# Two block levels of the scan's inverses on TensorE, and TensorE in program order

## The chip, the cores and the metric

The kernel runs on one core of a Trainium2 chip. The metric is the device time of one launch in microseconds; the time before is 3900.61 us, the median of three runs (3896.09 to 3906.93). The engines go by the profile's names: PE is TensorE (matmul, PEld its weight loads), DVE VectorE, ACT ScalarE, POOL GpSimd, SP the engine that issues most DMAs. Each works through its own list of instructions in order, and semaphores hold an instruction back until what it reads is there.

## What the kernel computes

A trunk of two layers over 512 latent and 256 context tokens of width 1024. Each layer is a half-weighted SwiGLU, a token mixer, and another SwiGLU; the second layer's mixer is a bidirectional RWKV-7, and only its recurrence is touched here. Of the reference:

```
def step(s, inp):                       # rwkv_scan, per head, both directions
    dec, kt, vt, kkt, bt = inp[:5]
    sa = jnp.einsum('bhvk,bhk->bhv', s, kkt)
    s = s * dec[:, :, None, :] - sa[..., None] * bt[:, :, None, :] \
        + vt[..., None] * kt[:, :, None, :]
    y = jnp.einsum('bhvk,bhk->bhv', s, inp[5]) if with_out else None
    return s, y
```

Sixteen heads of width 64; every latent scan starts from the final context state of its direction.

## The kernel before

The function `rwkv_scan` (L1181) does the recurrence in chunks of 64 tokens. Inside a chunk the dependence of each token on those before it is a triangular 64x64 matrix N, and what is needed is the inverse of (1 - N), called Y. The work comes in 12 stages, the list `todo`: four quads of four heads (`qd`), each with three groups of four chunks (`g`): 0 is the context, 1 and 2 the latents, for both directions at once. Below, item n is `todo[n]` and stage n is the pass of the loop at L1555 that scans item n.

For an item there are five steps. Each is a generator, and its `yield`s are the points at which the loop turns to another one.

- `prep_a` (L1225) loads K, R and B, forms the decays (`sw`, `cum` on PE, E and Ei on ACT), scales on DVE (KR L1278, BK L1281), multiplies to get the A blocks (PE L1304), masks them out of PSUM into N and Ar (DVE L1310), transposes N (`NT`, DVE L1315) and writes N's 32x32 diagonal blocks to DRAM as `md` (8 SP DMAs, L1318; four of them read N and four NT).
- `prep_m` (L1323) loads `md` as 64 partitions of 32x32 (M, L1330), inverts them on POOL by 30 steps of a multiply and an add (L1336, L1337), and writes `me` (L1340).
- `prep_d` (L1344) brings `me` back to SBUF as P1 (8 SP DMAs, L1350). `prep_c` (L1386) transposes P1 on DVE (PT, L1391) and joins the 32x32 inverses to the 64x64 Y on PE (TT L1409, Yo L1411).
- `prep_b` (L1352) loads V, transposes BK on PE by a matmul with the identity (`turned`, L295) and forms W.
- `scan` (L1430): four steps a stage, each a chain from engine to engine: kG (PE) -> rhs (DVE) -> U (PE, with Y) -> VU (ACT) -> G (PE) -> two DVE instructions on G -> the next kG, with the output y (PE) beside it. `readout` (L1497) normalises a finished quad.

While stage i scans, the loop interleaves `prep_a` of item i+2, and `prep_b`, `prep_d` and `prep_c` of item i+1. That is the order of the program. The order on each engine is made at compile time: a scheduler keeps a timeline of its own and issues, of the instructions that it believes ready, those of highest priority (`urgent` raises it: the scan and `prep_c`, `prep_d` by 800, `prep_a` by 400). Once compiled, the order is fixed, and an instruction whose input comes later than the scheduler believed holds up all behind it on its engine. POOL does nothing in the scan but the inversions.

Of the kernel before, what the change touches and what calls it, by code (L numbers as in the profile page):

```python
# [9 lines left out]
F32 = mybir.dt.float32  # L10
# [16 lines left out]
NQ1, NQ2 = 13, 15  # L27
RM, RP, RO, RV, RF = 3.0, 5.0, 0.3, 1.5, 1.3
# [10 lines left out]
TR = 2  # L39
# [11 lines left out]
SEQ = 'Adabc'  # L51
# [17 lines left out]
NCST = 790  # L69
# [4 lines left out]
def trunk(ctx, tc, io, phases=None, dump=None):  # L74
# [1105 lines left out]

    def rwkv_scan(l):  # L1181
# [5 lines left out]
        masks = [cst2[:, 260 + 128 * d:388 + 128 * d] for d in range(2)]  # L1187
        PP = open_psum("PP")
# [24 lines left out]
        diagonal = [[B1.tile([128, 16, 64], F32, name=f"P1_{i}{d}") for d in range(2)] for i in range(2)]  # L1213
        for d in range(2):
            dve.memset(diagonal[0][d], 0.0)
            pool.memset(diagonal[1][d], 0.0)
# [5 lines left out]
        lanes = [(d, hp, b, d * 32 + (hp * 2 + b) * 8, 64 * hp + 32 * b) for d in range(2) for hp in range(2) for b in range(2)]  # L1222
        ready, inverse = {}, {}

        def prep_a(qd, g):  # L1225
# [11 lines left out]
            for d in range(2):  # L1237
                t0 = starts(g)[d]
                kr = Q("KR")[:, :1024]
# [7 lines left out]
                lds.append(ld)  # L1247

                p = bank("sw", "a")
                for m in range(2):  # L1250
                    pe.matmul(p[:, 256 * m:256 * m + 256], hw[:, d, 128 * m:128 * m + 128],
                              low[qd][:, d], start=True, stop=True)
                sg = B1.tile([128, 512], F32, tag="sg", name="sg", bufs=2)
                act.activation(sg, p, AF.Tanh, scale=0.5)
                dve.tensor_scalar(sg, sg, 0.5, 0.5, ALU.mult, ALU.add)
                sgs.append(sg)
                yield
            for d in range(2):
# [10 lines left out]
                yield  # L1269
            for d in range(2):  # L1270
                E, Ei = EEs[d]
                ld = lds[d]
                ex, inc = (0, 1) if d == 0 else (1, 0)
                end, beg = (64, 0) if d == 0 else (0, 64)
                BK[d] = Q("BK").rearrange("p (c s n) -> p c s n", s=2, n=64)
                for i, o in ((0, ex), (1, inc))[:1 + lat]:
                    x = KR[d][:, :, i]
                    FE.tensor_tensor(x, x, E[:, :, o:o + 64], ALU.mult)  # L1278
                    yield
                for i in range(2):  # L1280
                    FE.tensor_tensor(BK[d][:, :, i], ld[:, i].rearrange("p e (c n) -> p (e c) n", n=64), Ei[:, :, inc:inc + 64], ALU.mult)  # L1281
                    yield
# [11 lines left out]
                yield  # L1294
            for d in range(2):
# [4 lines left out]
                for e in range(2):  # L1300
                    for hp in range(2):
                        p = bank("A", "a")
                        for c in range(4):
                            pe.matmul(p[:, 128 * c:128 * c + cols], BK[d][half(hp), 4 * e + c].rearrange("p s n -> p (s n)"),  # L1304
                                      KR[d][half(hp), 4 * e + c][:, :1 + lat], start=True, stop=True)
                        pv = p.rearrange("p (c s n) -> p c s n", s=2, n=64)
# [5 lines left out]
                        yield  # L1312
# [3 lines left out]
            md = dram.tile([64, 32, 32], F32, tag="md", name="md", bufs=2)  # L1316
            for d, hp, b, l0, r0 in lanes:
                nc.sync.dma_start(out=md[l0:l0 + 8].rearrange("l s t -> s l t"),  # L1318
                                  in_=(N[0] if d == 0 else NT_)[r0:r0 + 32, 8 * hp:8 * hp + 8, 32 * b:32 * b + 32])
            ready[qd, g] = KR, BK, N, Ar, gt, gs, md  # L1320
            yield

        def prep_m(qd, g):  # L1323
# [4 lines left out]
            me = dram.tile([64, 32, 32], F32, tag="me", name="me", bufs=2)  # L1328
            M = Q("M")[0:64, :1024].rearrange("l (s t) -> l s t", t=32)
            pool.dma_start(out=M, in_=md)  # L1330
            eng = ME
            mt = B1.tile([64, 256], F32, tag="mt", name="mt", bufs=2)
            for j in range(30, 0, -1):
                n = 31 - j
                t = mt[:, :j * n].rearrange("l (a b) -> l a b", b=n)
                eng.tensor_tensor(t, M[:, 0:j, j:j + 1].to_broadcast([64, j, n]), M[:, j:j + 1, j + 1:32].to_broadcast([64, j, n]), ALU.mult)  # L1336
                eng.tensor_tensor(M[:, 0:j, j + 1:32], M[:, 0:j, j + 1:32], t, ALU.add)  # L1337
                yield
            eng.memset(M.rearrange("l s t -> l (s t)")[:, 0:1024:33], 1.0)
# [4 lines left out]
        def prep_d(qd, g):  # L1344
            while (qd, g) not in inverse:
                yield
            me = inverse[qd, g]
            P1 = inverse[qd, g] = diagonal[(3 * qd + g) % 2]
            for d, hp, b, l0, r0 in lanes:
                nc.sync.dma_start(out=P1[d][r0:r0 + 32, 8 * hp:8 * hp + 8, 32 * b:32 * b + 32], in_=me[l0:l0 + 8].rearrange("l s t -> s l t"))  # L1350

        def prep_b(qd, g):  # L1352
# [9 lines left out]
            for d in range(2):  # L1362
                BKT[d] = Q("BKT").rearrange("p (e c n) -> p e c n", e=2, c=4)
                for e in range(2):
# [4 lines left out]
                    yield  # L1369

            W = Q("W").rearrange("p (i n) -> p i n", i=4)
            for i2 in range(2):
# [10 lines left out]
                yield  # L1383
            ready[qd, g] = KR, N, Ar, BKT, VU, W, gt, gs

        def prep_c(qd, g):  # L1386
            KR, N, Ar, BKT, VU, W, gt, gs = ready[qd, g]
            P1 = inverse.pop((qd, g))
            PT = [late["B2"].tile([128, 16, 32], F32, tag="PT0", name="PT0", bufs=1), Q("PT").rearrange("p (s n) -> p s n", n=64)]
            for d in range(2):  # L1390
                dve.transpose(PT[d], P1[d][:, :, :32 + 32 * d])  # L1391
                yield
            Y = [P1[0], PT[1]]

            tt = late["B2"].tile([128, 256], F32, tag="tt", name="tt", bufs=1)
            pt, py = bank("TT"), bank("Yo")
            for stage in range(2):
                for e in range(2):
                    for c in range(4):
                        for d in range(2):  # L1400
                            for hp in range(2):
                                s = slot(hp, e, c)
                                lo = 32 * (s % 8)
                                a = 64 * hp + 32 * d
                                b = 64 * hp + 32 * (1 - d)
                                ca, cb_ = 32 * d, 32 * (1 - d)
                                if stage == 0:
                                    other = (PT[0] if d == 0 else P1[1])[a:a + 32, s, ca:ca + 32]
                                    pe.matmul(pt[b:b + 32, lo:lo + 32], N[d][a:a + 32, s, cb_:cb_ + 32], other, start=True, stop=True, tile_position=(a, b))  # L1409
                                else:  # L1410
                                    pe.matmul(py[a:a + 32, lo:lo + 32], tt[b:b + 32, lo:lo + 32], Y[d][b:b + 32, s, cb_:cb_ + 32], start=True, stop=True, tile_position=(b, a))  # L1411
                    yield
                if stage == 0:
                    act.activation(tt, pt[:, :256], AF.Copy)
            for d in range(2):
                for hp in range(2):
                    a = 64 * hp + 32 * d
                    src = py[a:a + 32, :256].rearrange("p (s n) -> p s n", n=32)
                    dst = Y[d][a:a + 32, 8 * hp:8 * hp + 8, 32 * (1 - d):32 * (1 - d) + 32]
# [5 lines left out]
            yield  # L1425
# [4 lines left out]
        def scan(qd, g, KR, Ar, BKT, VU, Y, W, gt, gs):  # L1430
# [9 lines left out]
            for i in range(4):  # L1440
# [13 lines left out]
                for d, e in DE:  # L1454
                    for hp in range(2):
                        pe.matmul(p[half(hp), at(d, e)], Y[d][half(hp), slot(hp, e, cs[d])], rhs[half(hp), at(d, e)], start=True, stop=True)  # L1456
# [5 lines left out]
                if g < 2 or i < 3:  # L1462
# [12 lines left out]
                    yield  # L1475
                else:
                    new = None
                if lat:
                    p = bank("y", "s")
                    for d, e in DE:  # L1480
                        for hp in range(2):
                            pe.matmul(p[half(hp), at(d, e)], VU[:, d, cs[d], hp, e], Ar[d][:, slot(hp, e, cs[d])], start=True, stop=False)  # L1482
                        for hp in range(2):
                            pe.matmul(p[half(hp), at(d, e)], G[half(hp), 2 * d + e], KR[d][half(hp), 4 * e + cs[d], 1], start=False, stop=True)  # L1484
# [8 lines left out]
                    yield  # L1493
# [48 lines left out]
        second = prep_a(*todo[1])  # L1542

# [10 lines left out]
        inversions = chain(*(prep_m(*k) for k in todo[1:]))  # L1554
        for i, k in enumerate(todo):  # L1555
            ahead = stage(prep_a, i + 2)
            ahead = urgent(ahead, HP[1])
            parts = {"A": islice(ahead, 2), "a": ahead, "b": stage(prep_b, i + 1), "c": urgent(stage(prep_c, i + 1), HP[2]), "d": urgent(stage(prep_d, i + 1), HP[2])}
            prep = chain(*(parts[x] for x in SEQ))
            due = [0.0] * 3  # L1560
            for _ in urgent(scan(*k, *ready.pop(k)), HP[0]):
                for n, (f, r) in enumerate(((inversions, RM), (prep, RP), (out, RO))):
                    due[n] += r
                    while due[n] >= 1.0:
                        due[n] -= 1.0
                        next(f, None)
            for _ in prep:
                next(inversions, None)
            if k[1] == 2:
                for _ in out:  # L1570
                    pass
                out = readout(k[0], state["y"], to_dram)
# [141 lines left out]
def host_inputs(x, c, ctx, c_ctx, norm_w, mod_w, mod_b, ffn_w_in, ffn_w_out,  # L1714
# [18 lines left out]
    for d in range(2):  # L1733
# [6 lines left out]
        cst[:, 598 + 128 * d:662 + 128 * d] = (t <= c) if d == 0 else (t >= c)  # L1740
    lv = np.stack([(i[:, None] // (2 * b) == i // (2 * b)) & (i[:, None] // b != i // b) for b in (1, 2, 4, 8, 16, 32, 64)], 1)
# [20 lines left out]
```

## Times and profile before

| | |
|---|---|
| median of 3 runs | 3900.61 us |
| the profiled execution | 3901.05 us, its span 3899.3 us |
| busy: PE, DVE, ACT, POOL | 91%, 65%, 34%, 35% of the span |
| granted TensorE clock, mean | 0.926 of full |
| scan stages | about 2850 to 3427 us of the span |

The page gives each engine's busy share of the span and in 40 slices. [...] A matmul in float32 leaves two records in the trace, a transpose on PE one. The word "idle" in a row is the time for which the engine stood still just before, with what released it.

### The profile page before, as it was taken

How to read it: one execution, taken by the hardware profiler on the slowest of the kernel's cores; microseconds unless marked ns; L12 is line 12 of the kernel's file. 1: busy time of each engine (PE TensorE's matmuls, PEld its weight loads, DVE VectorE, ACT ScalarE, POOL GpSimd, SP SyncE). 2: the span in 40 equal slices, each digit the busy share in tenths (PEclk: the TensorE clock that was granted, in tenths of full speed). 3: DMA queues.
4: the chain of work that ended last, by engine and by line, in shares of the span. 5: the costliest groups of instructions: out<-in, count | busy, mean ns of one | idle time of the engine just before them, and what ended most of it. 6: DMA issues, size and time to landing. Idle time of an engine off the chain costs nothing. (4 is left out here: it accounts for less than half of the span.)

```text
span 3899.3 us, 61645 instructions
## 1 busy us (share of the span) xinstructions
PE 3551.6 (91%) x24898; PEld 3115.9 (80%) x24898; DVE 2529.3 (65%) x4042; ACT 1310.4 (34%) x2024; POOL 1382.0 (35%) x1395
## 2 busy tenths in 40 slices
PE   5999998899999899999899999698978889889998
PEld 3898997688888688888799998576867777668887
DVE  6766667656666866666766675776444554468886
ACT  4332333232322432333532333354322222244343
POOL 4212213433433422122422221522366766523332
PEclk9999999999999899999999999798967776779999
DMA  5332331411112233333132332247633332233332
GB/s 186 115 96 88 97 98 44 114 43 44 39 44 66 66 113 103 103 110 113 52 95 82 90 95 78 66 155 240 164 88 81 83 82 63 61 106 91 94 93 81
DMA packets 517051, 362.52 MB, mean 93 GB/s; under 512 B 83517, under 2 KB 490333, under 8 KB 516766
## 3 DMA queue, kind: packets, MB, share of 16 engines
q1 hardware_dynamic: 513694, 350.19, 30.5%
q0 software_dynamic: 1920, 6.29, 0.7%
q8 instruction: 196, 3.21, 0.3%
q10 hardware_dynamic: 1152, 2.10, 0.2%
q14 instruction: 89, 0.73, 0.1%
HBM read 315.64 MB, written 42.87 MB: 92 GB/s over the span
## 5 line engine op out<-in xcount | busy, mean ns | idle before, releaser
L607 PE MATMUL po<-g,whi 128*128 128x512 f32 (+1 forms) x2464 | 593.4, 350 | 10.2 <-ACT g L211 10.2
L551 POOL TENSOR_TENSOR raw<-raw 128x512 f32<-128x512 f32 x88 | 124.9, 1419 | 1341.3 <-DMA raw<-in_ffn_w_in 772.4
L534 PE MATMUL c<-u,whi 128*128 128x386 f32 (+1 forms) x2112 | 524.5, 332 | 48.1 <-DVE uu L565 15.9
L526 ACT ACTIVATE whi<-raw 128x1024 fp32r<-128x1024 f32 x352 | 332.5, 950 | 570.4 <-PE po L607 306.9
L607 PEld LDWEIGHTS po<-g,whi 128*128 128x128 f32 x2464 | 406.2, 190 | 84.6 <-issue 11.4
L527 DVE TENSOR_TENSOR wlo<-raw,whi 128x1024 fp32r<-128x1024 f32 x352 | 416.4, 1187 | 32.3 <-ACT whi L526 30.6
L534 PEld LDWEIGHTS c<-u,whi 128*128 128x128 f32 x2112 | 371.6, 191 | 76.2 <-ACT u L446 25.1
L534 PE MATMUL a<-u,whi 128*128 128x386 f32 (+1 forms) x1408 | 347.4, 331 | 23.6 <-DVE u L428 17.2
L607 PE MATMUL po<-g,wlo 128*128 128x512 f32 (+1 forms) x1232 | 367.1, 348 | 0.0
L611 DVE SCALAR_TENSOR_TENSOR h<-po,mod,h 128x512 f32<-128x512 f32 (+1 forms) x384 | 228.3, 628 | 194.3 <-PE po L607 194.2
L534 PE MATMUL b<-u,whi 128*128 128x386 f32 (+1 forms) x1408 | 344.1, 329 | 2.3 <-ACT pp L562 1.4
L534 PE MATMUL c<-u,wlo 128*128 128x386 f32 (+1 forms) x1056 | 344.9, 327 | 0.0
L534 PEld LDWEIGHTS a<-u,whi 128*128 128x128 f32 x1408 | 251.8, 192 | 29.0 <-issue 18.4
L196 ACT ACTIVATE whi<-raw 128x1024 fp32r<-128x1024 f32 (+1 forms) x193 | 184.7, 959 | 266.8 <-PE c L534 108.5
L534 PEld LDWEIGHTS b<-u,whi 128*128 128x128 f32 x1408 | 246.5, 189 | 12.3 <-issue 6.6
L197 POOL TENSOR_TENSOR wlo<-raw,whi 128x1024 fp32r<-128x1024 f32 x48 | 127.0, 2647 | 302.7 <-ACT whi L196 284.1
L534 PE MATMUL a<-u,wlo 128*128 128x386 f32 (+1 forms) x704 | 233.1, 331 | 0.5 <-DVE wlo L527 0.5
L607 PEld LDWEIGHTS po<-g,wlo 128*128 128x128 f32 x1232 | 208.0, 190 | 29.8
L534 PE MATMUL b<-u,wlo 128*128 128x386 f32 (+1 forms) x704 | 229.2, 326 | 1.0 <-DVE wlo L527 1.0
L1336 POOL TENSOR_TENSOR mt<-M 64x168 f32<-64x168 f32 (+5 forms) x360 | 191.7, 533 | 67.6 <-DMA M<-md 41.2
L1337 POOL TENSOR_TENSOR M<-M,mt 64x168 f32<-64x168 f32 (+5 forms) x360 | 199.6, 555 | 26.4
L534 PEld LDWEIGHTS c<-u,wlo 128*128 128x128 f32 x1056 | 203.5, 193 | 0.0
(362 smaller groups left out, 7295.2 us busy)
## 6 DMA issues: line engine op xcount, KB each, us to landing
raw<-in_ffn_w_in SPq DMA_DIRECT2D x176, 512.0 KB
raw<-in_mod_w SPq DMA_DIRECT2D x144, 512.0 KB
raw<-in_ffn_w_out SPq DMA_DIRECT2D x80, 384.0 KB
raw<-in_hgrn_w_in SPq DMA_DIRECT2D x40, 512.0 KB
raw<-in_ffn_w_out SPq DMA_DIRECT2D x28, 512.0 KB
raw<-in_w_rkv SPq DMA_DIRECT2D x24, 512.0 KB
ld<-s_bk SPq DMA_DIRECT2D x48, 256.0 KB
s_bk<-knb SPq DMA_DIRECT2D x32, 192.0 KB
```

The lines of the kernel that those rows point to most:

```text
L196: act.activation(hi[:, :m], raw[:, :m], AF.Copy)
L197: slots["lo"].tensor_tensor(lo[:, :m], raw[:, :m], hi[:, :m].bitcast(F32), ALU.subtract)
L526: act.activation(hi, x, AF.Copy)
L527: dve.tensor_tensor(lo, x, hi.bitcast(F32), ALU.subtract)
L534: pe.matmul(p[:, :q], a[:, c], x[k][:, b], start=first and k == 0 and i == 0, stop=k == 3 and i == 2, skip_group_check=not first)
L551: pool.tensor_tensor(S[:, lo], U[:, lo], U[:, hi], ALU.add)
L607: pe.matmul(p[v][:, :t1 - t0], wx[:, k, at:at + 128], x[:, e, t0:t1], start=k == 0 and i == 0, stop=k == nk - 1 and i == 2)
L611: dve.scalar_tensor_tensor(h[d][:, t0:t1], p[v][:, :t1 - t0], mods[l, sub, 2][:, d, v:v + 1], h[d][:, t0:t1], ALU.mult, ALU.add)
L1336: eng.tensor_tensor(t, M[:, 0:j, j:j + 1].to_broadcast([64, j, n]), M[:, j:j + 1, j + 1:32].to_broadcast([64, j, n]), ALU.mult)
L1337: eng.tensor_tensor(M[:, 0:j, j + 1:32], M[:, 0:j, j + 1:32], t, ALU.add)
```

## The change

`prep_m` now starts from 16x16 diagonal blocks, 128 of them on 128 partitions, so 14 steps on smaller tiles. `prep_a` writes, and `prep_d` reads, 16 DMAs in place of 8, each of half as many rows of 16 elements. `prep_c` then joins 16 to 32 (T16 and R16, 64 products of 32x32 each on PE, with a masking multiply, an add and a transpose on DVE) before TT and Yo join 32 to 64. The loop of the stages runs with PE in the program's order; DVE, ACT, POOL and SP stay with the scheduler. Further edits: the two heads of a pair alternate in the A products, four instructions each into a PSUM bank of its own, and both banks are taken at once; BK is transposed by PE's transpose mode; y's products of one kind come together; the `yield`s of the preparation carry weights, and each scan step is followed by a fixed share of their sum; the loads of `prep_a` for item i+3 are issued at the end of stage i.

```
-RM, RP, RO, RV, RF = 3.0, 5.0, 0.3, 1.5, 1.3
+RM, RO, RV, RF = 2.0, 0.45, 1.5, 1.3
-TR = 2
+TR = 6
+WORK = 14.0
...
                 for e in range(2):
+                    ps_ = [bank("A", "a") for _ in range(2)]
+                    for c in range(4):
+                        for hp in range(2):
+                            pe.matmul(ps_[hp][:, 128 * c:128 * c + cols], BK[d][half(hp), 4 * e + c].rearrange("p s n -> p (s n)"),
+                                      KR[d][half(hp), 4 * e + c][:, :1 + lat], start=True, stop=True)
...
-            md = dram.tile([64, 32, 32], F32, tag="md", name="md", bufs=2)
+            md = dram.tile([128, 16, 16], F32, tag="md", name="md", bufs=2)
...
-            for j in range(30, 0, -1):
-                n = 31 - j
+            mt = B1.tile([128, 64], F32, tag="mt", name="mt", bufs=2)
+            for j in range(14, 0, -1):
+                n = 15 - j
...
             for d, hp, b, l0, r0 in lanes:
-                nc.sync.dma_start(out=P1[d][r0:r0 + 32, 8 * hp:8 * hp + 8, 32 * b:32 * b + 32], in_=me[l0:l0 + 8].rearrange("l s t -> s l t"))
+                o = 16 * (b % 2)
+                nc.sync.dma_start(out=X[r0:r0 + 16, d, d, :, o:o + 16], in_=me[l0:l0 + 8].rearrange("l s t -> s l t"))
...
             for d in range(2):
-                dve.transpose(PT[d], P1[d][:, :, :32 + 32 * d])
-                yield
+                dve.transpose(X[:, 1 - d, d].rearrange("p s n -> p (s n)"), X[:, d, d].rearrange("p s n -> p (s n)"))
+            yield 0.01
...
+                        pe.matmul(p[a:a + 32, d, c], N[d][a:a + 32, 8 * hp + c, 32 * b:32 * b + 32], X[a:a + 32, 1, d, c], start=True, stop=True, tile_position=(a, a))
+            dve.tensor_tensor(t16.rearrange("p d s n -> p (d s) n"), p.rearrange("p d s n -> p (d s) n"), off16.unsqueeze(1).to_broadcast([128, 16, 32]), ALU.mult)
...
+                        pe.matmul(p[a:a + 32, d, c], t16[a:a + 32, d, c], X[a:a + 32, 0, d, c], start=True, stop=True, tile_position=(a, a))
+            A, AT = tile_of("A32"), tile_of("AT32")
+            dve.tensor_tensor(flat(A), flat(X[:, 0]), flat(p), ALU.add)
+            dve.transpose(flat(AT), flat(A))
...
+            prep = chain(islice(ahead, 2), islice(b, 2), islice(ahead, 2), b, d, ahead, islice(third, 1), c)
+            steps, total, done = (8 if k[1] == 0 else 12), WORK, 0.0
+            with tc.manual_schedule(engines={mybir.EngineType.PE}):
+                for n, _ in enumerate(urgent(scan(*k, *ready.pop(k)), HP[0])):
...
+                    while done < total * (n + 1) / steps:
+                        w = next(prep, None)
...
+                        done += w
```

DVE before, from the end of item 4's `prep_a` on: N and Ar are the evictions of A, NT the transpose that `md` waits for, PT the transpose of the inverse of item 3 come back from DRAM (P_10), sg and KR the scaling work of item 5.

```order
L1310 TENSOR_TENSOR N<-A,cst_21938 128x256
L1310 TENSOR_TENSOR Ar<-A,cst_21938 128x256
L1315 STREAM_TRANSPOSE NT<-N 128x1024
L1255 TENSOR_SCALAR sg<-sg 128x512 x2
L1391 STREAM_TRANSPOSE PT_24547<-P_10_21948 128x512
L1471 TENSOR_TENSOR G<-G 128x256
L1472 TENSOR_TENSOR G<-G,gt 128x256
L1492 TENSOR_TENSOR ybuf<-ybuf,y 128x2x64 x2
```

DVE now, from the end of item 3's `prep_a` on: X_1 is the inverse of that same item 3 come back from DRAM; t, A and AT are the new work of item 2.

```order
L1323 STREAM_TRANSPOSE NT<-N 128x1024
L1479 TENSOR_TENSOR rhs<-kG,W 128x256
L1415 TENSOR_TENSOR t_24276<-T_24277,cst_21938 128x512
L1423 TENSOR_TENSOR A_24408<-X_0_21946,R_24343 128x512
L1424 STREAM_TRANSPOSE AT_24409<-A_24408 128x512
L1502 TENSOR_TENSOR G<-G 128x256
L1503 TENSOR_TENSOR G<-G,gt 128x256
L1469 TENSOR_TENSOR G<-G,gs 128x256
L1479 TENSOR_TENSOR rhs<-kG,W 128x256
L1453 COPY Y_21948<-Yo 32x8x32 x2
L1262 TENSOR_SCALAR sg<-sg 128x512
L1402 STREAM_TRANSPOSE X_1_21947<-X_1_21947 128x256
```

Before, the NT of the next item (4) stands ahead of the transposes of an item's inverse (3); now an item's own X follows its own NT after 11 instructions, and the next item's NT comes behind it. These are the DVE instructions that follow, the second half of X_1 and then the scaling work of item 4, whose A products and NT come after it.

```order
L1402 STREAM_TRANSPOSE X_1_21947<-X_1_21947 128x256
L1502 TENSOR_TENSOR G<-G 128x256
L1503 TENSOR_TENSOR G<-G,gt 128x256
L1523 TENSOR_TENSOR ybuf<-ybuf,y 128x2x64 x2
L1285 TENSOR_TENSOR KR<-KR,E 128x512 x2
L1299 COPY gt<-E 128x2
L1288 TENSOR_TENSOR BK<-ld,Ei 128x8x64
L1295 TENSOR_TENSOR gt<-E,Ei 128x2x3
L1288 TENSOR_TENSOR BK<-ld,Ei 128x8x64
L1300 COPY gs<-Ei 128x2
```

All of the scaling work of item 4, and the scan's own G, stand behind the second X_1 transpose. On PE, before, a latent stage's A products lie in pieces among bkt, sw and the scan's U, G and kG:

```order
L1304 MATMUL A<-KR,BK 128x128 x3
L295 MATMUL bkt<-cst,BK 128x128 x4
L1304 MATMUL A<-KR,BK 128x128 x4
L1456 MATMUL U<-rhs,P_10_21948 64x64 x4
L1456 MATMUL U<-rhs,PT 64x64 x4
L1304 MATMUL A<-KR,BK 128x128 x8
L1466 MATMUL G<-VU,BKT 64x64 x8
L1304 MATMUL A<-KR,BK 128x128 x4
L1251 MATMUL sw<-w_s,hw_s 128x256 x2
```

On PE now, the same place of a latent stage:

```order
L1390 MATMUL W<-VU,N 64x64 x16
L1477 MATMUL kG<-G,KR 64x64 x8
L1311 MATMUL A<-KR,BK 128x128 x16
L1486 MATMUL U<-rhs,Y_21948 64x64 x8
L1311 MATMUL A<-KR,BK 128x128 x8
L1497 MATMUL G<-VU,BKT 64x64 x8
L1512 MATMUL y<-Ar,VU 64x64 x8
L1515 MATMUL y<-KR,G 64x64 x8
L1311 MATMUL A<-KR,BK 128x128 x8
```

The A products now stand in four rounds of eight behind a kG, and each round needs both of its PSUM banks emptied by DVE.

## Rows read from the trace of the kernel before

**Rows 1.** Windows, the scan: us, then busy us (instructions) by engine, clock, DMA.
```profile
2860.00:3427.00 567.00, 479.65 (x6517) 402.91 (x6518) 266.30 (x605) 137.69 (x333) 362.15 (x683) 0.73 0.29 73
```
**Rows 2.** Waits in the scan: engine, line, waited for; us in total, times, longest.
```profile
DVE PT L1391 <- DMA P<-me: 80.5, 13, 12.7
SPq L1243 <- PE y L1482: 50.6, 3, 18.5
```
**Rows 3.** Timeline, one round of the inversion: start us, us, engine, line, instruction.
```profile
3091.59 0.24 POOL L1336 TENSOR_TENSOR mt<-M 64x30 f32<-64x30 f32 x1 [2.64 <-DMA M<-md]
...
3129.29 0.59 POOL L1340 DMA_DIRECT2D me<-M  x1 [0.29 <-POOL M L1337]
3132.22 3.75 SPq L1350 DMA_DIRECT2D P<-me  x8
3135.03 0.71 DVE L1391 STREAM_TRANSPOSE PT<-P 128x512 f32<-128x512 f32 x1 [12.56 <-DMA P<-me]
...
3138.21 2.09 SPq L1318 DMA_DIRECT2D md<-NT  x4
3142.39 0.52 POOL L1330 DMA_DIRECT2D M<-md  x1 [12.52 <-DMA hw_s<-s_hw]
3145.89 0.24 POOL L1336 TENSOR_TENSOR mt<-M 64x30 f32<-64x30 f32 x1 [2.99 <-DMA M<-md]
```
**Rows 4.** Timeline, DVE: the NT of items 2, 5 and 11, and one PT.
```profile
2873.61 1.23 DVE L1315 STREAM_TRANSPOSE NT<-N 128x1024 f32<-128x1024 f32 x1
...
2994.00 1.24 DVE L1391 STREAM_TRANSPOSE PT<-P 128x1024 f32<-128x1024 f32 x1
...
3026.29 1.23 DVE L1315 STREAM_TRANSPOSE NT<-N 128x1024 f32<-128x1024 f32 x1
...
3337.75 1.23 DVE L1315 STREAM_TRANSPOSE NT<-N 128x1024 f32<-128x1024 f32 x1
```
**Rows 5.** Groups by form on POOL: shapes, count, busy us, mean ns, idle before.
```profile
L1337 POOL TENSOR_TENSOR M<-M,mt 64x58 f32<-64x58 f32 x21 | 6.6, 314 | 0.7
...
L1337 POOL TENSOR_TENSOR M<-M,mt 64x30 f32<-64x30 f32 x21 | 5.1, 245 | 1.5
```
**Rows 6.** Groups by line in the scan: DVE and ACT, same columns.
```profile
L1460 ACT ACTIVATE VU<-U 64x256 f32<-64x256 f32 x94 | 35.6, 378 | 128.1 <-PE U L1456 126.5
...
L1281 DVE TENSOR_TENSOR BK<-ld,Ei 128x512 f32<-128x512 f32 x37 | 33.0, 926 | 9.3 <-PE bkt L295 5.3 <-PE y L1484 4.0
L1310 DVE TENSOR_TENSOR N<-A,cst 128x256 f32<-128x256 f32 x80 | 32.7, 419 | 38.2 <-PE A L1304 35.7 <-POOL M L1337 2.1
...
L1278 DVE TENSOR_TENSOR KR<-KR,E 128x512 f32<-128x512 f32 x30 | 24.4, 835 | 20.1 <-DMA KR<-s_kk 19.4 <-DMA KR<-s_r 0.7
...
L1472 DVE TENSOR_TENSOR G<-G,gt 128x256 f32<-128x256 f32 x40 | 19.5, 487 | 1.3
...
L1492 DVE TENSOR_TENSOR ybuf<-ybuf,y 128x128 f32<-128x128 f32 x30 | 7.2, 282 | 10.6 <-PE y L1484 10.6
```
**Rows 7.** Groups by line in the scan: PE, same columns.
```profile
L1304 PE MATMUL A<-KR,BK 64*128 64x128 f32 (+1 forms) x624 | 82.2, 360 | 9.4 <-DVE BK L1281 4.9 <-DVE Ar L1310 2.4 <-DVE gs L1293 1.2
...
L295 PE MATMUL bkt<-cst,BK 128*128 128x128 f32 x336 | 59.5, 340 | 0.4 <-ACT PT L1421 0.3 <-DVE ybuf L1522 0.2
```
**Rows 8.** Timeline, PE: A and kG runs at either level of the clock.
```profile
2975.24 3.09 PE L1304 MATMUL A<-KR,BK 64*128 64x128 f32 x16
...
3119.03 0.68 PE L1447 MATMUL kG<-G,KR 64*64 64x64 f32 x16
...
3122.21 1.71 PE L1304 MATMUL A<-KR,BK 64*128 64x128 f32 x16
```
**Rows 9.** Windows: TT alone (PE, PEld, ACT); then all engines, vT transposes, PE idle.
```profile
3098.70:3099.60 0.90, 0.75 (x64) 0.64 (x64) 0.00 (x0) 1.00 0.00 0
...
2754.50:2756.00 1.50, 1.50 (x13) 1.42 (x12) 0.24 (x1) 1.33 (x2) 0.00 (x0) 1.00 0.75 184
3132.00:3134.00 2.00, 0.00 (x0) 0.00 (x0) 0.00 (x0) 0.00 (x0) 0.00 (x0) 0.50 0.20 30
```

More of the change, by code (lines that the diff above doesn't have):

```diff
@@ L50 @@
 HP = 800, 400, 800
-SEQ = 'Adabc'
 Q1 = ("KR", "BK", "Ar")
@@ L68 @@
 NV = V_C + 16
-NCST = 790
+NCST = 822
 @with_exitstack
@@ L1211, in decay_weights @@
             nc.sync.dma_start(out=w2[64:65], in_=io["w0"][:, 256 * qd:256 * qd + 256].unsqueeze(0))
[L1213 to L1216, printed above, removed]
+        diagonal = [B1.tile([128, 2, 2, 8, 32], F32, name=f"X16_{i}") for i in range(2)]
+        whole = [B1.tile([128, 2, 8, 64], F32, name=f"Y_{i}") for i in range(2)]
+        for x in diagonal:
+            dve.memset(x, 0.0)
+        for x in whole:
+            pool.memset(x, 0.0)
         FE, ME = dve, pool
@@ L1221, in rwkv_scan @@
         starts = lambda g: ((TL, TL), (0, 256), (256, 0))[g]
-        lanes = [(d, hp, b, d * 32 + (hp * 2 + b) * 8, 64 * hp + 32 * b) for d in range(2) for hp in range(2) for b in range(2)]
+        lanes = [(d, hp, b, d * 64 + (hp * 4 + b) * 8, 64 * hp + 16 * b) for d in range(2) for hp in range(2) for b in range(4)]
         ready, inverse = {}, {}
@@ L1247, in prep_a @@
                 lds.append(ld)
+            yield 0.01
+            for d in range(2):
                 p = bank("sw", "a")
@@ L1300, in prep_a @@
                 for e in range(2):
-                    for hp in range(2):
[L1302 to L1306, printed above, removed]
+                    ps_ = [bank("A", "a") for _ in range(2)]
[3 more added lines that the diff above has]
+                                      KR[d][half(hp), 4 * e + c][:, :1 + lat], start=True, stop=True)
+                    for hp in range(2):
+                        pv = ps_[hp].rearrange("p (c s n) -> p c s n", s=2, n=64)
                         s0 = slot(hp, e, 0)
@@ L1397, in prep_c @@
             for stage in range(2):
[L1398 to L1412, printed above, removed]
+                for c in range(8):
+                    for d in range(2):
+                        for hp in range(2):
+                            lo = 32 * c
+                            a = 64 * hp + 32 * d
+                            b = 64 * hp + 32 * (1 - d)
+                            if stage == 0:
+                                pe.matmul(pt[b:b + 32, lo:lo + 32], N[d][a:a + 32, 8 * hp + c, 32 * (1 - d):32 * (1 - d) + 32], AT[a:a + 32, d, c], start=True, stop=True, tile_position=(a, b))
+                            else:
+                                pe.matmul(py[a:a + 32, lo:lo + 32], tt[b:b + 32, lo:lo + 32], A[b:b + 32, d, c], start=True, stop=True, tile_position=(b, a))
                 if stage == 0:
                     act.activation(tt, pt[:, :256], AF.Copy)
+                    yield 0.5
             for d in range(2):
@@ L1455, in scan @@
                     for hp in range(2):
-                        pe.matmul(p[half(hp), at(d, e)], Y[d][half(hp), slot(hp, e, cs[d])], rhs[half(hp), at(d, e)], start=True, stop=True)
+                        pe.matmul(p[half(hp), at(d, e)], Y[half(hp), d, 4 * e + cs[d]], rhs[half(hp), at(d, e)], start=True, stop=True)
                 for hp in range(2):
@@ L1461, in scan @@
                 yield
-                if g < 2 or i < 3:
+                last = g == 2 and i == 3
+                if not last:
                     p = bank("G", "s")
@@ L1479, in scan @@
                     p = bank("y", "s")
-                    for d, e in DE:
+                    for n, (d, e) in enumerate(DE):
                         for hp in range(2):
-                            pe.matmul(p[half(hp), at(d, e)], VU[:, d, cs[d], hp, e], Ar[d][:, slot(hp, e, cs[d])], start=True, stop=False)
+                            pe.matmul(p[half(hp), at(d, e)], VU[:, d, cs[d], hp, e], Ar[d][:, slot(hp, e, cs[d])], start=n == 0, stop=True, skip_group_check=n > 0)
+                    for n, (d, e) in enumerate(DE):
                         for hp in range(2):
-                            pe.matmul(p[half(hp), at(d, e)], G[half(hp), 2 * d + e], KR[d][half(hp), 4 * e + cs[d], 1], start=False, stop=True)
+                            pe.matmul(p[half(hp), at(d, e)], G[half(hp), 2 * d + e], KR[d][half(hp), 4 * e + cs[d], 1], start=False, stop=True, skip_group_check=True)
                     for d in range(2):
@@ L1542, in rwkv_scan @@
         second = prep_a(*todo[1])
+        inversions = chain(*(prep_m(*k) for k in todo[1:]))
         def prologue():
@@ L1553, in rwkv_scan @@
             pass
-        inversions = chain(*(prep_m(*k) for k in todo[1:]))
+        third = stage(prep_a, 2)
+        next(third)
         for i, k in enumerate(todo):
[L1556 to L1572, printed above, removed]
+            ahead = urgent(third, HP[1])
+            third = stage(prep_a, i + 3)
+            b, c, d = stage(prep_b, i + 1), urgent(stage(prep_c, i + 1), HP[2]), urgent(stage(prep_d, i + 1), HP[2])
+            prep = chain(islice(ahead, 2), islice(b, 2), islice(ahead, 2), b, d, ahead, islice(third, 1), c)
+            steps, total, done = (8 if k[1] == 0 else 12), WORK, 0.0
+            due = [0.0] * 2
+            with tc.manual_schedule(engines={mybir.EngineType.PE}):
+                for n, _ in enumerate(urgent(scan(*k, *ready.pop(k)), HP[0])):
+                    for m, (f, r) in enumerate(((inversions, RM), (out, RO))):
+                        due[m] += r
+                        while due[m] >= 1.0:
+                            due[m] -= 1.0
+                            next(f, None)
+                    while done < total * (n + 1) / steps:
+                        w = next(prep, None)
+                        if w is None:
+                            break
+                        done += w
+                for _ in prep:
+                    next(inversions, None)
+                if k[1] == 2:
+                    for _ in out:
+                        pass
+                    out = readout(k[0], state["y"], to_dram)
         close("PS", "B1")
```

74 lines of the change are left out of this document (46 added, 28 removed).

## The prediction

> **What bounds the kernel now.** I read the windows first, to find the stretch that the change touches and which engine is full there; then the waits, the timeline of one inversion, and last the groups, for prices. The windows show that in the scan PE is busy 479.65 of 567 us, 85%, at a mean clock of 0.73 [rows 1]. That looks like a PE bound, but the waits say otherwise: DVE stood still for 80.5 us in front of PT, for inverses that had not come back from DRAM [rows 2].
>
> The timeline gives the loop. From the first multiply of an inversion (3091.59) to its `me` store (3129.29) POOL needs 37.7 us. Then come 2.9 us to the first P load, 2.8 us to the first PT, 3.2 us to the `md` stores of the next item (its NT and its SP issues stand right behind), 4.2 us to the load of M and 3.5 us to the next inversion's first multiply (3145.89): 54.3 us a round [rows 3]. Over items 2 to 11 the NT transposes lie 3337.75 - 2873.61 = 464.1 us apart in nine rounds, 51.6 each [rows 4]; where the next `md` was ready early, a round is shorter. So POOL's inversion and the hops around it set the pace, and PE's 85% is work done beside it, much of it at the lower clock.
>
> What lies beside the inversion matters as much. Between a PT and the next NT stands the next item's scaling, its A products and their evictions: in one stage PT ends at 2995.24 and NT ends at 3027.52, 32.3 us [rows 4]. Before, that stretch runs while POOL inverts.
>
> **The change part by part.** *The inversion.* 60 instructions on POOL become 28, with j(15-j) elements each, 14 to 56, 40 on the mean. Between the rows for 30 elements (245 ns) and 58 (314 ns), 40 cost 0.27 us, and 1.5 us of idle in 21 is 0.07 each [rows 5]: 28 x 0.34 = 9.5 us for 37.7, 28 us less a round. No row has 128 partitions: if an instruction is no dearer than at 30 elements and 64 partitions, 8.8; if twice the partitions double it, 17. I take 9.5.
>
> *The hops.* Four more `md` issues behind NT at 2.09/4 = 0.52 us make 4.2 into 6.3; the M load stays 3.5, `me` 2.9. X has 16 issues at 3.75/8 = 0.47 for 8: its first direction is in SBUF 2.8 + 4 x 0.47 = 4.7 us after the first issue, the second after 2.8 + 12 x 0.47 = 8.4 [rows 3]. From NT to the first X transpose: 6.3 + 3.5 + 9.5 + 2.9 + 4.7 = 26.9 us, to the second 30.6.
>
> *The place of X on DVE.* This decides. In the new order DVE comes to X_1 eleven instructions after NT of the same item: three small G's, two rhs, two Y copies and sg at 0.4 to 0.5 us (N's and G's rows), t, A and AT at 0.8 (KR's row) [rows 6], and between them PE's T16, R16, TT and Yo: 64 records in a run took 0.75 us [rows 9], so 4 x 0.75 for the two new products and 1.5 for the old ones. That is some 11 us. X is there after 26.9. DVE then stands for about 16 us, and for most of another 3.7 before the second half, and behind it stand the scan's own G and rhs, so PE runs dry as well. And KR, BK, the A evictions and NT of the next item now come behind X: the stretch that lay beside the inversion joins the loop.
>
> *That stretch.* For a latent item DVE does X 0.4, six G at 0.49, six ybuf at 0.28, four KR at 0.84, four BK at 0.93, eight small copies (at ybuf's 0.28), two rhs and sixteen N and Ar at 0.42, NT 1.2: 23.0 us. A context item (no r, no Ar, no ybuf, but sg) has 16.8 [rows 4, 6]. On top come the waits in it. U, two VU and G: 0.68 + 2 x 0.38 + 0.68 = 2.1 us, and a kG of 0.68. Then four rounds of A, each behind the eviction of the last, since both banks are taken at once: 1.71 each at the full clock, half of that for a context item. Together 9.6 and 6.2 us; at the lower level PE's part is 3.09/1.71 = 1.8 times as long, 16.7 and 10.6 [rows 6, 8]. If the alternating heads run wholly side by side, A halves: 6.2 for the latent item. So the stretch is 29 to 40 us for a latent item, 21 to 27 for a context one; the measured 32.3 stands among them, and I take 34 and 24.5, since PE falls to the lower level when it stands still (clock 0.50 from 3132 to 3134, with no matmul in it) [rows 9].
>
> *The other edits on PE.* The A products side by side and BK by transposes save at most half of 82.2 + 59.5 us [rows 7], T16 and R16 add 11 x 3.0 us; y is regrouped. Where DVE holds the loop these lie in time in which PE waits: nothing, save the A rounds already counted. PE's program order adds no wait of its own that is longer than DVE's.
>
> Transposes on PE do not by themselves show a fall of the clock: the stretch with the transposes of v among dense matmuls is at 1.00 [rows 9]. [...]
>
> **The sum.** Rounds: 30.6 + 34 = 64.6 us latent, 30.6 + 24.5 = 55.1 context. Items 3 to 11 are six latent and three context: 6 x 64.6 + 3 x 55.1 = 553 us, against 464. The time before item 2's NT and that after item 11's I leave as they are: the first inversion is 28 us shorter, but beside the value products; then item 1's round is longer; at the end two stages stand behind the last X where one did (-15 to +20 us together). 3901.05 + 89 = 3990 us; the profiled execution is within 0.5 us of the median, so no correction.
>
> **The rivals.**
> A. *The loop is at its floor.* If DVE's own work fills the stretch and nothing waits in it, rounds are 53.6 and 47.4 us: 6 x 53.6 + 3 x 47.4 = 464, and the time is 3900. For it: PE in order clears its A products without other work between; against: U, VU, G and each A round do hand over.
> B. *X is hidden and PE bounds.* If X is there when DVE comes to it, the inversion is off the path. PE then has 479.65 - 70.9 + 33 = 442 us; at the share (85%) and clock of before that is 522 us of scan, 3856; at the full clock 442 x 0.73/0.85 = 380, 3714. For it: 28 us less on POOL. Against: it needs 30 us between NT and X on DVE, where the order has 11. I put it at 3830.
> C. *SP holds `md` up.* In the new order a KR load of a later item stands between the `md` stores of N and of NT, and it waits for a buffer that the running scan frees; before, such waits took 50.6 us in three, up to 18.5 [rows 2]. If it costs 8 us a round, nine make 72: 4062. For it: the queue is in order; against: the buffer may be one that is free by then.
>
> [...]
>
> **How the numbers follow.** My case 0.50 (3945 to 4035 as the stretch goes from 30 to 40 us), C and dearer inversions 0.20, A 0.09, B 0.21. What a measurement of this kernel can tell from no change is 0.3%, about 12 us. Faster is B: 0.21. Same is most of A, 0.07. Slower is the rest, 0.72. The range for 8 in 10 runs from 3840, which leaves out the deeper half of B, to 4070.
>
> **What would show it.** Right: DVE waits in front of the X transposes, L1402, for the loads from `me`, some 14 to 20 us an item and 150 us or more in all; NT to NT 52 to 68 us; POOL busy in the scan falls from 362 us to about 100 with long idle; PE's busy share there falls well under 85%, with a clock no better than 0.73. Wrong: if L1402 waits less than 5 us an item and stages follow each other in 45 us or less, B holds. If rounds are near 52 us with DVE dense, A. If the wait is in SP at L1248, C.

## The result, and the profile after

The changed kernel takes 3957.56 us, the median of four runs (3953.98 to 3960.20), against 3902.75 for the kernel before beside it: ratio 1.0141, 95% interval 1.0124 to 1.0159. It is slower, inside the range, 32 us under the 3990 forecast. The profiled span is 3955.4 us against 3899.3. One of the ten runs of the kernel called *chain cut up* below took 14935.69 us; its ratio leaves that run out, and the median of the other nine is 3886.60.

The windows of the scan after, with the columns of [rows 1]:

```profile
2880.00:3483.00 603.00, 424.97 (x9209) 359.12 (x9208) 245.09 (x645) 164.97 (x374) 87.99 (x310) 0.74 0.24 60
```

POOL fell from 362 us to 88, PE from 85% busy to 70%, the clock stayed where it was (0.73, now 0.74), and the stretch grew from 567 to 603 us.

Waits in the scan after (2860 to 3480), which answer to [rows 2]:

```profile
POOL M L1338 <- DMA md<-NT: 410.4, 10, 49.7
DVE X L1402 <- DMA X<-me: 141.1, 20, 12.5
...
PE U L1486 <- DVE rhs L1479: 52.9, 23, 7.0
...
PE cum L1271 <- DVE sg L1262: 27.4, 4, 9.2
...
PE U L1486 <- DVE Y L1453: 20.3, 5, 11.5
```

POOL, which paced the scan, now waits; DVE stands for X where it stood for PT, for longer; and PE waits for rhs (52.9 us, before 12.2), sg and Y, three DVE instructions that are queued around the standing X.

One round of the timeline after, from item 9's NT to item 11's, as [rows 3, 4] show it of before:

```profile
3279.08 1.25 DVE L1323 STREAM_TRANSPOSE NT<-N 128x1024 f32<-128x1024 f32 x1
...
3343.72 1.23 DVE L1323 STREAM_TRANSPOSE NT<-N 128x1024 f32<-128x1024 f32 x1
...
3344.98 4.35 SPq L1326 DMA_DIRECT2D md<-NT  x8
...
3351.42 0.54 POOL L1338 DMA_DIRECT2D M<-md  x1 [49.68 <-DMA md<-NT]
...
3354.96 0.21 POOL L1344 TENSOR_TENSOR mt<-M 128x14 f32<-128x14 f32 x1
...
3364.81 0.59 POOL L1348 DMA_DIRECT2D me<-M  x1 [0.30 <-POOL M L1345]
3366.86 7.43 SPq L1359 DMA_DIRECT2D X<-me  x16
3372.10 0.45 DVE L1402 STREAM_TRANSPOSE X<-X 128x256 f32<-128x256 f32 x1 [12.52 <-DMA X<-me]
...
3373.00 2.07 PE L1271 MATMUL cum<-cst,sg 128*128 128x130 f32 x8 [9.18 <-DVE sg L1262]
3375.79 0.45 DVE L1402 STREAM_TRANSPOSE X<-X 128x256 f32<-128x256 f32 x1 [2.48 <-DMA X<-me]
3376.16 1.25 DVE L1285 TENSOR_TENSOR KR<-KR,E 128x512 f32<-128x512 f32 x2
...
3393.86 1.23 DVE L1323 STREAM_TRANSPOSE NT<-N 128x1024 f32<-128x1024 f32 x1
```

The inversion takes 9.9 us (3354.96 to 3364.81). From the end of item 10's NT to the second X transpose it is 30.8 us, 15.0 of them standing in two pieces; only then come KR and the rest of item 11's preparation, 17.6 us to its NT. The round before, item 9 to 10, was 64.6 us, this one 50.1.

Where the 56.1 us of the span are: NT of item 2 comes at 2894.45, 20.8 us later than before; from there to NT of item 11 it is 499.4 us in place of 464.1, 35.3 more; what follows takes 561.5 us in both.

### The profile page after: what moved, and what is told of

It reads as the page before. It is cut to its first block, busy times and chain, and to the rows that moved or that the text cites. A ratio compares the mean times of both kernels' runs of the same rounds, so it can differ in the third digit from the quotient of the medians.

```text
span 3955.4 us, 67263 instructions
## 1 busy us (share of the span) xinstructions
PE 3491.5 (88%) x27778; PEld 3068.5 (78%) x27778; DVE 2498.5 (63%) x4078; ACT 1341.5 (34%) x2072; POOL 1092.5 (28%) x1011
## 4 chain that ended last, share of the span: by engine, by line
PE 32%; DVE 8%; DMA 3%; POOL 3%; SPq 2%; issue 2%; ACT 1%; POOLq 0%; DVEq 0%; ACTq 0%
PE po L607 8%; PE c L534 5%; PE a L534 4%; PE b L534 3%; PE v L222 1%; PE A L1311 1%; PE k L222 1%; SPq L1359 1%; POOL M L1345 1%; POOL mt L1344 1%; SPq L1326 1%; PE o L222 1%; DVE wlo L527 1%; DMA M<-md 1%; DVE mx L960 1%
## 5 line engine op out<-in xcount | busy, mean ns | idle before, releaser
L197 DVE TENSOR_TENSOR wlo<-raw,whi 128x768 fp32r<-128x768 f32 (+1 forms) x145 | 171.7, 1185 | 36.5 <-ACT whi L196 36.2
L316 POOL TENSOR_TENSOR nsq<-nsq 128x768 f32<-128x768 f32 (+1 forms) x49 | 102.0, 2082 | 221.0 <-ACT nsq L314 198.0
```

The costliest lines, as they stand in the source:

```text
L197: slots["lo"].tensor_tensor(lo[:, :m], raw[:, :m], hi[:, :m].bitcast(F32), ALU.subtract)
L316: pool.tensor_tensor(sq[:, :n], acc[:, :n], sq[:, :n], ALU.add)
```

## The experiments

The theory was the prediction's: DVE works in order, so X standing in its queue puts the round trip and the next item's preparation in one loop. The rivals: PE's program order, the clock, the inversion itself. A "round" below is the distance of the NT of items 2 and 11 over nine. L1402 is the line of the X transposes, "stood" the time for which DVE waited there for the loads from `me`. In the rows T and R are the products T16 and R16, and t is the masking multiply between them; "at A" means at the products that give the A blocks (L1311).

**X moved out of the way, and a control.** In both kernels DVE follows program order as PE does; the second has the transposes ahead of the next item's preparation.

```
-            with tc.manual_schedule(engines={mybir.EngineType.PE}):
+            with tc.manual_schedule(engines={mybir.EngineType.PE, mybir.EngineType.DVE}):
     control also:
-            prep = chain(..., b, d, ahead, islice(third, 1), c)
+            prep = chain(..., b, d, islice(c, 1), ahead, islice(third, 1), c)
```

> VectorE follows program order in the scan as TensorE does; by that order the two X transposes of an item (L1402) stand right behind the NEXT item's NT transpose instead of 10 to 20 instructions behind their own. Theory (the X transposes stand in the in-order VectorE queue for the round trip NT, md, inversion, me, X, and the next item's KR, BK and mask products queue behind them): the waits of L1402 on the X loads, 154.8 us in the changed kernel, fall under 30 us; NT to NT falls from 55.5 us a round to what TensorE needs (425 us busy in 603 us of the scan window is 39 us a round, with the chain T, R, TT, Yo at the end of an item 42 to 46); nine or ten rounds give 90 to 130 us: 3840 us (3800 to 3890). Rival 1, TensorE's program order or its clock is what costs: nothing changes on TensorE, so 3945 to 3970. Rival 2, VectorE in program order is itself a cost (evictions of the scan wait behind the preparation): 3980 or more.

> The control: VectorE in program order too, but the X transposes are written ahead of the next item's preparation (10 instructions behind their own NT, as in the changed kernel). Theory: the standing comes back, L1402 waits 100 to 170 us in all, NT to NT 53 to 60 us a round, 3950 us (3920 to 3990), some 100 us above the kernel with the late X. Rival 2b, it is VectorE's program order as such and not the place of X that decides: the same time as the kernel with the late X within 20 us.

Late X: 3942.04 us, ratio to before 1.0121 (1.0102 to 1.0140). Control: 3947.99, 1.0127 (1.0108 to 1.0146). X stood 15.0 us in all with late X, as foreseen, and the time hardly moved; rival 1's 3945 to 3970 came nearest. The control missed too: with 11 to 34 instructions between NT and X, not 10, X stood only 23.9 us. Neither waits for X, both have rounds of 54 to 55 us, so something else held them. The waits of PE with late X, from 2880 to 3440:

```profile
PEld A L1311 <- DVE BK L1288: 31.3, 9, 4.0
...
PE A L1311 <- DVE BK L1288: 28.0, 9, 3.7
...
PE T L1414 <- DVE X L1402: 24.2, 11, 2.7
```

PE (and its weight load, over the same gaps) waits at A for BK, since KR and BK are written behind `bkt` and W and in program order come only when A is due.

**The inversion twice as long, in each of the two.** Each step of the inversion is done once more into a scratch tile.

```
+            Ms = B1.tile([128, 16, 16], F32, tag="Ms", name="Ms", bufs=1)
+            for j in range(14, 0, -1):
...
+                eng.tensor_tensor(Ms[:, 0:j, j + 1:16], M[:, 0:j, j + 1:16], t, ALU.add)
```

> As the control with early X, and GpSimd does each of the 14 steps of the inversion once more into a scratch tile before the real ones (28 instructions, 9.9 us more of the round trip). Theory (the round trip is in the loop): every round grows by 9.9 us, eleven rounds, some 90 to 110 us above the control: 4050 us. Rival 3 (the inversion no longer paces anything since it became short): within 15 us of the control.

> The same doubled inversion in the kernel with late X. Theory: the round trip of 31 us, now 41, lies beside a whole round of 42 us or more, so nothing or little changes: 0 to +20 us against the kernel with late X. Rival 4 (the inversion paces the scan wherever X stands): +90 to +110 us here as well.

With early X 4006.14 us, ratio 1.0285 (1.0268 to 1.0302), 58 us above its control: rounds of 60.4 for 55.0, X stood 95.1 us for 23.9. With late X 3934.04, 1.0097 (1.0078 to 1.0117), no slower than without. So the round trip is in the loop where X is early and out of it where X is late; of the 9.9 us a round, 5.4 came through. That the control's rounds had slack at X fits its 23.9 us of standing.

**PE's order, the clock, and KR and BK earlier.** Four kernels:

```
 no PE order (the changed kernel; no engine in program order):
-            with tc.manual_schedule(engines={mybir.EngineType.PE}):
+            if True:
 fill (late X, with products that nobody reads in PE's gaps):
+        def fill(n):
+            p = bank("fill")
+            for _ in range(n):
+                pe.matmul(p, blk128, cst2[:, 0:512], start=True, stop=True)
...
 KR early (late X; KR and BK right behind cum):
+            pre = 2 * (4 + (todo[i + 2][1] > 0)) if i + 2 < len(todo) else 0
-            prep = chain(islice(ahead, 2), islice(b, 2), islice(ahead, 2), b, d, ahead, ..., c)
+            prep = chain(islice(ahead, 2), islice(b, 2), islice(ahead, 2), islice(ahead, pre), b, d, ahead, ..., c)
 chain cut up (as KR early, and then):
+            ... b, d, islice(ahead, 2), islice(c, 2), islice(ahead, 1), islice(c, 1), islice(ahead, 1), islice(c, 1), ahead, ..., c)
```

> The 16-blocks alone: the changed kernel without TensorE's program order in the scan; by the scheduler's order the X transposes stand 15 to 35 VectorE instructions behind their own NT, 10 to 30 ahead of the next. Where the two first pairs of runs leave it: taking the X standing out of VectorE's queue freed only 6 to 16 us, with TensorE at 75% busy and a granted clock of 0.69, so a second limit lies right under the first. Theory 2 (in program order TensorE has gaps, ahead of A for BK and in the chain T, R, TT, Yo, and behind such gaps the clock is low: 342 of 560 us in the kernel with late X): with other work let into the gaps the granted clock rises over 0.75 and the time falls to 3880 us (3840 to 3920). Rival (TensorE's order is not what costs, the X transposes in VectorE's queue are): 3945 to 3990 us, L1402 waits over 100 us.

> The kernel with late X, and TensorE gets 12 matmuls of 128x512 that nobody reads for each item, written into its known gaps (3 ahead of the first A group and 1 ahead of each of the other three, 2 ahead of T, 1 ahead of R, 2 ahead of TT, 1 ahead of Yo). One such takes 1.12 us at full clock by the row of the readout's mean. Theory 2 (the gaps bring the clock down, and the clock is the second limit): the granted clock of the scan goes from 0.69 to 0.85 or more, an item needs some 27 us of work at full clock and 13 for these, rounds of 42 to 48 us against 54: 3860 us (3800 to 3920). Rival (TensorE is bound by its work at whatever clock, or the clock does not answer to gaps): 12 items of 13 to 26 us more: 4080 us or above, clock 0.65 to 0.72.

> The kernel with late X, and the KR and BK products of the item after next are written right behind its cum, ahead of the rest of bkt and W, so VectorE does them while TensorE has bkt and W to do; no work is added. Theory 2: the waits of A on BK (59 us on TensorE and its weight load in the kernel with late X) go to under 15 us, one of the gaps of a round with them, clock 0.72 to 0.80, 3900 us (3860 to 3930). Rival (another gap takes over or the clock does not answer): 3930 to 3950.

> As the one before, and the chain X, T, R, TT, Yo is cut up between the A groups (A, A, X and T, A, R, A, TT, NT, Yo), so that each wait of the chain has an A group under it. Theory 2: the gaps ahead of T, R, TT and Yo shrink, clock 0.75 to 0.85, 3860 us (3810 to 3915). Rival (the X transposes are early again, some 40 VectorE instructions behind their NT, and the standing is back): L1402 waits over 60 us, 3920 to 3960.

*No PE order*: 3904.78 us, 1.0014 (1.0003 to 1.0024), 53 us under the changed kernel with X still standing 133.4 us, and the clock at 0.77 (2880 to 3380): time and clock are the second theory's, the standing is its rival's. *Fill*: 3944.75, 1.0126 (1.0109 to 1.0143), against 3942.04 without. *KR early*: 3892.73, 0.9984 (0.9964 to 1.0003), rounds of 49.9. *Chain cut up*: 3887.75, 0.9967 (0.9956 to 0.9977), rounds of 49.0, and X stood 63.4 us with the clock at 0.74.

With fill the clock came as the second theory said, and the time did not. The windows of the kernel with late X:

```profile
2880.00:3380.00 500.00, 382.93 (x7650) 326.94 (x7648) 211.05 (x553) 138.96 (x318) 80.98 (x279) 0.70 0.25 63
```

And of the same with fill:

```profile
2880.00:3380.00 500.00, 430.84 (x7851) 305.53 (x7851) 208.93 (x547) 139.19 (x318) 81.57 (x279) 0.88 0.25 62
```

With the gaps filled the clock went from 0.70 to 0.88, but no time came of it, where 80 us were expected; nor did the filling cost the 138 of its rival. In this window the unread products took 121.7 of PE's 430.84 busy us, so PE's own work fell from 383 to 309 and the filling took more than that, part of it in what had been gaps. Whether a better clock without such a load would pay, or the rounds were held elsewhere, these two runs don't tell. That time can be had without the clock KR early shows: it freed 49 us with the clock at 0.69, where 0.72 or more was expected with it. PE's waits at A for BK, 28.0 us, were gone (1.5 us were left on its weight load). What it freed is more than these 28 us; the rest I can't place.

**The two together.** KR early, with the X transposes put back early (they move from `prep_c` into `prep_d`, and `d` goes ahead of KR):

```
-            prep = chain(..., islice(ahead, pre), b, d, ahead, islice(third, 1), c)
+            prep = chain(..., d, islice(ahead, pre), b, ahead, islice(third, 1), c)
```

> The kernel with early KR and BK (3892.73 us, X late), with one thing put back: the X transposes stand 10 VectorE instructions behind their own NT, ahead of the next item's KR and BK. Theory 3 (the standing at X and the products KR and BK late for A are two covers of the same length: with A's gap there, taking the standing away frees 6 to 16 us, and with A's gap gone the standing costs its full price): L1362 (the transposes' line here) waits 100 us or more, rounds of 55 to 60 us against 49.9, 3945 to 3985. Rival (the standing at X never cost much, TensorE's gap at A did): under 3915.

3933.99 us, 1.0096 (1.0081 to 1.0111): 41 us above KR early, rounds of 53.1 for 49.9, X stood 79.1 us. The expectation was 50 to 90, with 100 us or more of standing; the sign and the place are the theory's, the sizes are not. The four kernels make a square:

| us | KR, BK late | KR, BK early |
|---|---|---|
| X early | 3947.99 | 3933.99 |
| X late | 3942.04 | 3892.73 |

Each fault alone costs nearly the whole; mending one of the two gives 6 us (not clear of noise) or 14, mending both 55. The square is not strict: with KR, BK and X all early, the loads of X and X itself stand ahead of the rest of `prep_b` too, with 9 to 28 instructions between NT and X where the control had 11 to 34.

**Only DVE in program order.** The kernels with late X, and with KR early, with PE left to the scheduler:

```
-            with tc.manual_schedule(engines={mybir.EngineType.PE, mybir.EngineType.DVE}):
+            with tc.manual_schedule(engines={mybir.EngineType.DVE}):
```

> The kernel with late X, but only VectorE follows program order and TensorE's order is the scheduler's again. Theory: TensorE can take other work into the gap ahead of A and into the chain T to Yo, and no X stands in VectorE's queue: 3870 us (3840 to 3900), granted clock of the scan over 0.74. Rival (VectorE's program order, with KR and BK behind bkt and W, holds TensorE at A whatever TensorE's order): 3925 to 3945 as with late X.

> The kernel with early KR and BK, but only VectorE follows program order. Theory: gaps fewer still, 3870 us (3845 to 3895), the fastest or level with the kernel whose chain is cut up (3887.75). Rival (the scheduler puts ready preparation ahead of the scan's own matmuls, so the scan stands back): 3895 to 3930.

3940.02 us, 1.0111 (1.0093 to 1.0129), and 3910.05, 1.0036 (1.0021 to 1.0051). With DVE's order fixed, PE's program order costs nothing (3942.04 against 3940.02) or gains 17 us (3892.73 against 3910.05). Both rivals were right on the time. In the first kernel the place is another than the rival said: PE no longer waits long at A for BK (8 us), but the scheduler puts T late, and DVE stands at t instead. A row of its waits, from 2880 to 3440:

```profile
DVE t L1415 <- PE T L1414: 73.0, 11, 12.0
```

**A version that beats both.** The cut-up chain with the X transposes one A group later.

```
-                         ... islice(ahead, 2), islice(c, 2), islice(ahead, 1), islice(c, 1), islice(ahead, 1), islice(c, 1), ahead, ..., c)
+                         ... islice(ahead, 3), islice(c, 2), islice(ahead, 1), islice(c, 1), ahead, islice(third, 1), c)
```

> The kernel with early KR and BK and the cut-up chain, with the X transposes one A group later (A, A, A, X and T, A, R, NT, TT, Yo). Theory (in the first form L1402 stands 63.4 us for its loads and T waits some 50 us for it): both waits fall under 20 us, rounds of 46 to 48 us against 49.0, 3867 us (3845 to 3885). Rival (the clock, 0.74 in the scan of the first form, is what bounds it now): 3880 to 3895 with the standing gone.

3867.97 us, 0.9910 (0.9892 to 0.9927), rounds of 47.8. X stood 36.0 us in place of 63.4, not under 20; T waited some 25. DVE's timeline in one round, the X of item 10 between the NT of items 10 and 11:

```profile
3281.39 1.20 DVE L1323 STREAM_TRANSPOSE NT<-N 128x1024 f32<-128x1024 f32 x1
...
3314.97 0.43 DVE L1402 STREAM_TRANSPOSE X<-X 128x256 f32<-128x256 f32 x1
3317.13 0.45 DVE L1402 STREAM_TRANSPOSE X<-X 128x256 f32<-128x256 f32 x1 [1.73 <-DMA X<-me]
...
3324.52 1.24 DVE L1323 STREAM_TRANSPOSE NT<-N 128x1024 f32<-128x1024 f32 x1
```

DVE comes to the first X 32.4 us behind the end of NT and does not stand, waits 1.73 us for the second, and 7 us later the next NT follows: most of the preparation now lies ahead of X, beside the round trip.

## Why the prediction was right, and where it was off

- *The inversion and the hops.* 9.9 us for 9.5; 30.8 from NT to the second X for 30.6, and 30.2 to 32.6 over items 1 to 11. The issues took 4.35/8 = 0.54 us for `md` (0.52) and 7.43/16 = 0.46 for X (0.47).
- *The standing.* 154.8 us of L1402 over the whole scan for "150 us or more", 15.0 in the round shown for 16 + 3.7. POOL busy 88 us for about 100, PE 70%, clock 0.74 for "no better than 0.73".
- *The rounds.* Items prepared while a latent stage scans came out near the forecast: the three context items at 51.1, 54.1 and 55.7 us for 55.1, items 4, 7 and 10 at 58.5, 63.2 and 64.6 for 64.6. The mis-sized term is the stretch of 34 us for all six latent items. Items 5, 8 and 11 are prepared while a context stage scans, which has no y, no ybuf and fewer steps, so that between the second X and NT less stands: 17.6 us in the rows above. Their rounds were 52.0, 50.0 and 50.1, together 42 us below the forecast; the other six make another 12, and 553 - 54 is the 499 measured. I had priced the stretch by the item that is prepared and not by the stage that runs beside it: from the second X to NT, DVE was busy 19.5 of 30.9 us for item 10 and 13.1 of 17.6 for item 11. That items 7 and 10 come so close is in part luck. The sum left out the readout, 3.9 us of DVE in item 10's stretch, it had KR and BK too dear, and it took PE to be partly at the lower level, while the clock in the nine stretches was 0.78 to 1.00.
- *The start.* Left at -15 to +20, it was +20.8 by item 2. The end was left alone and did not change. So -54 + 21 = -33 is the whole error of the sum; that the two cancel in part is luck.
- *The dearer half of the argument.* That DVE's queue is what decides held, but I took the standing for the only thing in it. The square shows a second: where X does not stand, KR and BK, late in the same queue, cost as much. Rival B, "X is hidden", was priced at 3830 (3856 at the share and clock of before) on the ground that only PE would be left; X hidden alone gave 3942, and only with KR and BK moved and the chain cut up, 3868. So the sign of the forecast did not hang on X alone: with X out of the way, and DVE in program order, the kernel is still 1.2% slower than before.
- *PE's program order.* The prediction put it at nothing. In time that held where DVE's order was fixed and X late (3942.04 against 3940.02). Against the changed kernel, though, freeing PE gave 53 us, nearly all of the slowdown. There the scheduler also lays DVE out anew: from item 1 on 21 to 43 instructions stand between NT and X, where it was 7 to 22. Among them are all of the next item's KR and BK (in one round all but two), which from item 2 on all stood behind X in the changed kernel; so X still stands 133.4 us, but beside the round trip much of the preparation is done. That run doesn't separate PE's order from DVE's; by these rows and the pairs with DVE fixed I put it down to DVE's, which is argued and not shown.
- *The rivals A and C.* A's dense DVE was not seen: DVE was busy 245 of 603 us. C is refuted: SP's waits for y at the KR loads were 19.6 us in six, and in all ten rounds the `md` stores of NT were issued within 0.04 us of its end.
- *The clock.* BK now goes through PE's transposes, and the granted clock of the scan is 0.74, for 0.73 with products; what did move it were unread products in the gaps, from 0.70 with late X to 0.88. These transposes stand among other products, so the runs say nothing of transposes by themselves.

## What to carry to other kernels

Shortening the step that paces a loop pays only if the in-order queue that takes its result does not come to it before it is there: look up where the consumer stands in the new order, and count what is queued behind it, by the stage that runs beside it; here POOL's work in the scan fell from 362 us to 88 and the kernel took 1.4% longer. Where two instructions in one queue are badly placed, each covers the other, and undoing one alone shows next to nothing, here 6 or 14 us against 55 for both; try them as a square of four. A scheduler's order on one engine is part of what changes when another engine's is fixed: here DVE had 21 to 43 instructions between NT and X with PE free, for 7 to 22.

## What the runs showed of the hardware

DVE's products of two SBUF operands were faster while POOL was not inverting. Groups on DVE in the scan after, which answer to [rows 6]:

```profile
L1318 DVE TENSOR_TENSOR N<-A,cst 128x256 f32<-128x256 f32 x80 | 32.5, 419 | 35.2 <-PE A L1311 35.2
...
L1288 DVE TENSOR_TENSOR BK<-ld,Ei 128x512 f32<-128x512 f32 x38 | 25.8, 682 | 0.0
...
L1285 DVE TENSOR_TENSOR KR<-KR,E 128x512 f32<-128x512 f32 x32 | 20.7, 679 | 6.6 <-ACT E L1273 6.6
```

BK takes 682 ns for 926, KR 679 for 835, while N, which reads PSUM, stays at 419. In the kernel before, the same KR took this in the middle of an inversion (from 3091.59 to 3129.29, [rows 3]) and with POOL waiting for `md`:

```profile
3107.14 2.15 DVE L1278 TENSOR_TENSOR KR<-KR,E 128x512 f32<-128x512 f32 x2
...
3247.97 0.69 DVE L1278 TENSOR_TENSOR KR<-KR,E 128x512 f32<-128x512 f32 x1 [3.83 <-DMA KR<-s_kk]
```

1.08 us each against 0.69. From 2860 us on, 56 of the KR and BK before lie inside an inversion and take 0.89 and 0.95 us on the mean, up to 1.18; the 10 outside take 0.68 to 0.69. In the changed kernel none lies inside one, and the longest takes 0.69. The prediction had priced KR and BK at the slower figures.

The clock stood at one of two levels nearly all the time: of the 1400 windows of 0.4 us from 2860 to 3420 in the kernel before, 631 read 1.00 and 730 read 0.50, the prediction's full clock and its lower level; 39 read a mean of the two. With late X it fell behind a stretch in which PE did little. The timeline of PE with late X, at A behind the readout's mean:

```profile
3028.11 1.12 PE L1538 MATMUL mean<-ybuf,cst 128*128 128x512 f32 x2
...
3032.43 1.16 PE L1311 MATMUL A<-KR,BK 64*128 64x128 f32 x16 [3.19 <-DVE BK L1288]
3036.16 2.70 PE L1311 MATMUL A<-KR,BK 64*128 64x128 f32 x16 [2.57 <-DVE Ar L1318]
```

The windows there, clock in the third column from the end:

```profile
3030.00:3034.00 4.00, 1.16 (x16) 0.97 (x16) 4.00 (x10) 0.63 (x1) 0.00 (x0) 0.99 0.30 68
3034.00:3038.00 4.00, 1.84 (x12) 1.71 (x14) 2.67 (x11) 0.00 (x0) 0.00 (x0) 0.50 0.76 223
3038.00:3042.00 4.00, 3.54 (x40) 3.00 (x36) 2.38 (x7) 0.00 (x0) 0.00 (x0) 0.65 0.24 58
3042.00:3046.00 4.00, 2.19 (x32) 1.80 (x32) 2.88 (x8) 0.76 (x2) 0.00 (x0) 1.00 0.34 68
```

PE stood 3.19 us, worked 1.16 us at A and stood again; the clock fell at 3034, 0.4 us into that second gap. Sixteen records of A take 1.16 us ahead of the fall and 2.70 behind it, at a granted 0.50; by 3042 the clock is at 1.00 again.
